# DeltaNet projections all kept in two parts, and one direction's triangular inverses moved to GpSimd

## The chip, the cores and the metric

The kernel runs on one core of a Trainium2 chip. The metric is the device time of one execution in microseconds (us). Below, PE is TensorE, PEld its weight loads, DVE is VectorE, ACT is ScalarE, POOL is GpSimd and SP is SyncE; SP computes nothing here and only issues DMA. TensorE's clock is granted by the chip and has two levels, 1.2 and 2.4 GHz; the profile gives the mean granted clock of a stretch as a share of the full one.

## What is computed

The reference is a trunk of two layers over 256 context tokens and 256 latent tokens of width 1024. Each layer is a half-step SwiGLU feed-forward block (FFN, inner width 2816), a token mixer and a second FFN; the mixer of layer 0 is a gated linear recurrence (LRU), that of layer 1 a bidirectional gated DeltaNet with 8 heads. What matters here is the DeltaNet:

```python
proj = h @ w_in                                   # q, k, v: silu(conv4(.)), z, and a/b for decay and beta
q = l2norm(q) * DN_DK ** -0.5;  k = l2norm(k)
g = -exp(a_log) * softplus(a + dt_bias);  beta = sigmoid(b)
# per direction, chunk of 64 tokens and head:
g_cum = cumsum(g);  decay = exp(g_cum_i - g_cum_j)  for i >= j
a_mat = strictly_lower((k * beta) @ k.T * decay) + I
u, w = solve(a_mat, [v * beta, k * beta * exp(g_cum)])
# then a scan over the chunks with the state s:
v_new = u - w @ s;  o = q_dec @ s + (q @ k.T * decay) @ v_new;  s = s * g_tot + k_dec.T @ v_new
```

There are 64 unit lower triangular matrices a_mat of 64x64 (2 directions, 4 chunks, 8 heads). The output is the latent stream after the last RMSNorm.

## The kernel before

**Weights.** All large products take three matmuls (`mm3`, lines 300 to 303): weight and activation are each the sum of a high part (float32r) and the rest, and hi·hi, hi·lo and lo·hi are added up. A weight tile is 128x1024 floats (512 KB). `Weights` brings it in: SP loads it raw (tile `wr`), ACT makes the high part of each half of 512 columns (`split`, line 165, the trace's CAST), and DVE the low part (line 166). So a tile costs two ACT and two DVE instructions of 128x512. Some later tiles are instead split ahead of time: an entry `keep` in the plan has a tile split during an FFN, SP writes the four pieces to DRAM (tile `kp`), and when its turn comes it is loaded in two parts of 512 KB straight into the pair buffers `wp` (`load`, lines 200 to 212). Before, these loads are issued by POOL (line 209). `PACE["keep"]` says after which inner tiles j of the FFNs 0,1 and 1,0 an entry stands: "1j10 2j10" means after every second one, 22 places in all; `kept_from` and `kept_out` say which tiles use them: the last 16 of the 28 later projections and 4 output tiles.

**The DeltaNet** (`deltanet`). The first four projections (k heads 0 to 3) are made while the normed input arrives. The other 28 are a loop over a list (`SEQ`): k4 to k7, the 8 q heads, then v and z heads mixed in the order of `PACE["seq"]`. A k or v head projects all 512 tokens (two halves of 24 matmuls of 128x256), a q or z head the latent half only. After every six matmuls `tick` runs a few steps of generators that write the remaining work into the program: convolutions, `decays` (from projection number `decay_from`, counted from 0, drained at `decay_to`), and from `keys_from` one step of `keys`. `keys` runs, in this order: per head the key products and decay matrices (`k_rest`), the norms (`norms`), the inverses (`solve`) and the products that put the inverse together (`merge`). `PACE["solve"]` is the number of ticks per step of `solve`.

**The inverses.** `solve` inverts the two 32x32 diagonal blocks of every a_mat. 128 partitions hold 128 blocks of each direction. `N` gets the transposed blocks, `Bc` (its halves are `XI`) starts as the identity, and 31 steps j follow, each of two instructions: tm = column j of N times row j of Bc, and Bc -= tm below row j. Before, both directions are one instruction of 2·m·n elements a partition (n = j+1, m = 31-j), all on DVE (lines 1225 and 1228). Then DVE makes four transposes (lines 1231 and 1232: `A`, `N`, `Bc`), and `merge` starts: 256 matmuls of 32x32 (`pp`, line 1247), ACT copies them out, and for a = 0 and 1 another 128 each (`qq`, line 1266), from which `Yp[a]` is filled. `Yp[0]` takes the memory of the context half of the normed input, which is free after the last v projection (state "contexts"), `Yp[1]` that of the latent half, free after the last projection (state "latents"). Then come the transposes of the keys (`tk`, lines 1131 and 1136), and the scan.

**What sets the order.** In the DeltaNet a scheduler places the instructions of each engine; each engine then runs its own list strictly in order, and an instruction that waits holds up all that stand behind it on its engine. In the FFNs and the LRU the order of PE and SP at least is that of the code.

Of the kernel before, what the change touches and what calls it, by code (L numbers as in the profile page):

```python
# [10 lines left out]
F32 = mybir.dt.float32  # L11
# [4 lines left out]
OP = mybir.AluOpType  # L16
# [11 lines left out]

    "lru": "u0 u1 u2 u3 u4 u5 g0 u6 u7 g1 y0 y1 y2 g2 y3 y4 y5 g3 y6 y7",

    "seq": "qqqqqqqqvvvvzzvzzvvzzvzz",

    "decay_from": 6, "decay_to": 8, "keys_from": 9,

    "steps": 4, "decay_steps": 1, "key_every": 4, "key_steps": 3, "solve": 4, "q_lag": 2, "v_lag": 6, "k_lag": 4,

    "block_split": 1, "mo": 2,

# [2 lines left out]
    "ahead": 1,  # L41


    "kept_from": 12, "kept_out": 4, "keep": "1j10 2j10",
}


# [47 lines left out]
def trunk(ctx, tc, io):  # L95
    nc = tc.nc
# [84 lines left out]
    class Weights:  # L181
# [15 lines left out]
        def load(self, n, half=False):  # L197
            new = []
            while self.plan and len(self.raw) + len(self.ready) < n:
                src, m, *r = self.plan[0]  # L200
                if r == ["p"]:
                    if len(self.raw) + len(self.ready) >= self.limit:
                        break
                    self.plan.popleft()
                    d = self.kept[src]
                    parts = []
                    for a in range(2):
                        w = self.rings["g"].pair()
                        POOL.dma_start(w.both, d[:, a])
                        parts.append(w)  # L210
                    self.raw.append((parts, m, None, None))
                    continue
                if "l" not in self.rings and r == ["l"]:
                    break
                ring = self.rings["g" if r == ["g"] else self.raws[self.nr % len(self.raws)]]
                if ring.used == ring.nraw:
                    break
                if r == ["keep"]:
                    self.kept[src] = self.pool.tile([128, 2, 2, 512], F32R, name=nm("kp"), tag=nm("kp"))
                    r = ["keep", self.kept[src]]  # L220
                    src = io[src[0]][src[1:]]
                self.plan.popleft()
                self.nr += r != ["g"]
                raw = ring.raw()
                ring.used += 1
                nc.sync.dma_start(raw[:, :512 if half else m], src[:, :512] if half else src)
                self.raw.append((raw, m, ring, r))
                if half:
                    new.append((raw[:, 512:m], src[:, 512:]))
            return new  # L230
# [722 lines left out]
    def deltanet(norm, next_norm, sp, hp, pools, done):  # L953
# [258 lines left out]
        def solve():  # L1212
            Nb = pools[1].tile([128, 2, 32, 32], F32, name="N")
            N, XI = ([t[:, dr] for dr in range(2)] for t in (Nb, Bc))
            for dr in range(2):
                DVE.transpose(out=N[dr] if dr == 0 else N[dr].rearrange("p i e -> p e i"), in_=Bc[:, dr])
                x = XI[dr]
                POOL.memset(x, 0.0)
                POOL.memset(x.rearrange("p i c -> p (i c)")[:, ::33], 1.0)
                yield  # L1220
            for j in range(31):
                n, m = j + 1, 31 - j
                tm = pools[1].tile([128, 512], F32, name=nm("tm"), tag="tm", bufs=1)[:, :2 * m * n]
                tm = tm.rearrange("p (d i c) -> p d i c", d=2, c=n)
                DVE.tensor_tensor(tm, Nb[:, :, j + 1:, j:j + 1].to_broadcast([128, 2, m, n]),
                                  Bc[:, :, j:j + 1, :n].to_broadcast([128, 2, m, n]), OP.mult)
                x = Bc[:, :, j + 1:, :n]
                DVE.tensor_tensor(x, x, tm, OP.subtract)
                yield
            for dr, (A, B) in enumerate(((sv("A"), N[0]), (N[1], XI[0]))):  # L1230
                DVE.transpose(out=A.rearrange("p k c -> p c k"), in_=XI[dr].rearrange("p i c -> p c i"))
                DVE.transpose(out=B.rearrange("p k i -> p i k"), in_=XI[dr])
                T[dr], Yd[dr] = (A, B) if dr == 0 else (B, A)
                yield
# [4 lines left out]
        def merge():  # L1239
# [3 lines left out]
            for i0 in (0, 16):  # L1243
# [6 lines left out]
                ACT.copy(pt, pp)  # L1250
                PT.append(pt.rearrange("p (i x) -> p i x", i=16))
                yield
            for a in range(2):
                while a and "latents" not in state:
                    yield
                at = [(dr, c) for dr in range(2) for c in range(2) if a == (c if dr == 0 else 1 - c)]

                Yp.append(hp.tile([128, 32, 128], F32, name=nm("Yp"), tag=f"H{a}", bufs=1))
                (DVE if a else POOL).memset(Yp[a][:, 0:16], 0.0)
                POOL.memset(Yp[a][:, 16:32], 0.0)  # L1260
                for i0 in (0, 16):
                    ii = slice(i0, i0 + 16)
                    qq = bank("qq")
                    for i in range(16):
                        for dr, c in at:
                            PE.matmul(qq[ER[dr, c], i * 32:i * 32 + 32], PT[i0 // 16][IR[dr, c], i, :],
                                      Yd[dr][IR[dr, c], i0 + i, :], start=True, stop=True)
                    for dr, c in at:
                        for k in range(2):
                            dst, src = Yp[a][sub(c, k), ii, sub(c, k)], Yd[dr][sub(c, k), ii]  # L1270
                            if k == 0:
                                ACT.copy(dst, src)
                            else:
                                POOL.tensor_scalar(dst, src, 1.0, 0.0, OP.mult, OP.add)
                    yield
                    for dr, c in at:
                        r = ER[dr, c]
                        dst, src = Yp[a][r, ii, IR[dr, c]], qq[r, :].rearrange("p (i x) -> p i x", i=16)
                        if c:
                            ACT.activation(dst, src, AF.Identity, scale=-1.0)  # L1280
                        else:
                            DVE.tensor_scalar(dst, src, -1.0, None, OP.mult)
                    yield
# [16 lines left out]
        def keys():  # L1300
            live = Pipe()
            for n in range(8):
                while ("k", n) not in state:
                    yield
                live.live.append(k_rest(n))
                for _ in range(PACE["key_every"]):
                    live.tick(PACE["key_steps"])
                    yield
            while live.live:
                live.tick(3)  # L1310
                yield
            yield from norms()
            for _ in solve():
                yield from pause(PACE["solve"])
            while "contexts" not in state:
                yield
            yield from merge()

        later = keys()
# [440 lines left out]
```

## Time and profile before

| | |
|---|---|
| median of 3 runs | 1844.87 us (1843.44 to 1848.66) |
| profiled execution, its own time | 1852.49 us |
| its span, first to last instruction | 1850.7 us |
| mean granted TensorE clock | 0.984 |
| busy: PE, DVE, ACT, POOL | 1782.6, 1314.8, 809.1, 105.7 us |

Places in the trace are us from the span's start. By the rows of PE the FFN 0,1 runs from 594 to 953, the FFN 1,0 from 959 to 1317, the first four DeltaNet projections from 1322, the other 28 from 1349.4 to 1497.0, the pp and qq products to 1514, the scan from 1522, the last FFN from about 1642. A busy PE is no proof of a PE at its peak, because the ends of matmuls are modelled; the distance between starts says more. Durations of DVE instructions that follow each other overlap by some hundredths of a us where the second does not need the first.

### The profile page before, as it was taken

To read this page: it belongs to the slowest core of one execution; us is meant where nothing else is said; L and a number is where in the kernel's file an instruction comes from. 1 tells how busy PE (TensorE), PEld (TensorE's weight loads), DVE (VectorE), ACT (ScalarE), POOL (GpSimd) and SP (SyncE) were. 2 spreads that over 40 slices of the span, in tenths; PEclk is the share of its full clock that TensorE was granted. 3 is DMA by queue.
4 is the path that set the end of the run, shared out by engine and by line. 5 is a ranking of instruction groups with operands and counts; after the bars stand their busy time and mean duration, and the time that the engine had idled before them with its cause. 6 is when DMAs were issued, how large, how long until landed. Compare 5 with 4: busy or idle time off the path is not lost.

```text
span 1850.7 us, 28613 instructions
## 1 busy us (share of the span) xinstructions
PE 1782.6 (96%) x10806; PEld 1544.5 (83%) x10806; DVE 1314.8 (71%) x2694; ACT 809.1 (44%) x1661; POOL 105.7 (6%) x146
## 2 busy tenths in 40 slices
PE   5999999999899999999999999999998989889997
PEld 3788888888778888888898888888997986789997
DVE  7877866797878767667656755545789966976555
ACT  5532222346884433233334322323578333855453
POOL 3100000000000000000000000000017230100000
PEclk9999999999999999999999999999999989989999
DMA  9354645452133666576524765663235540035553
GB/s 346 113 183 158 218 160 172 166 197 80 57 103 127 236 203 219 194 235 213 193 88 151 231 227 199 216 201 127 87 119 167 184 137 1 1 128 178 194 182 106
DMA packets 98058, 300.59 MB, mean 162 GB/s; under 512 B 10880, under 2 KB 20352, under 8 KB 97792
## 3 DMA queue, kind: packets, MB, share of 16 engines
q1 hardware_dynamic: 92160, 277.79, 44.5%
q0 software_dynamic: 5760, 20.97, 3.6%
q8 instruction: 85, 1.39, 0.3%
q14 instruction: 53, 0.43, 0.1%
HBM read 276.70 MB, written 22.02 MB: 161 GB/s over the span
## 4 chain that ended last, share of the span: by engine, by line
PE 80%; DVE 10%; issue 4%; ACT 4%; DMA 2%; POOL 0%; SPq 0%; POOLq 0%; ACTq 0%; DVEq 0%
PE gu L302 14%; PE gu L303 14%; PE gu L301 14%; PE fo L303 4%; PE fo L301 4%; PE fo L302 4%; PE tl L301 4%; PE tl L302 4%; PE tl L303 4%; PE p L1417 1%; DVE u L791 1%; PE p L1406 1%; PE gu L546 1%; PE gu L542 1%; PE p L1386 1%
## 5 line engine op out<-in xcount | busy, mean ns | idle before, releaser
L165 ACT CAST wp<-wr 128x512 fp32r<-128x512 f32 (+1 forms) x689 | 382.4, 607 | 281.9 <-DMA wr<-in_ffn_out_dram 66.1
L166 DVE TENSOR_TENSOR wp<-wr,wp 128x512 fp32r<-128x512 f32 (+1 forms) x689 | 433.4, 675 | 99.7 <-ACT wp L165 95.8
L302 PE MATMUL gu<-hl,wp 128*128 128x512 f32 (+1 forms) x1312 | 479.3, 365 | 8.0 <-DVE hl L505 8.0
L301 PE MATMUL gu<-hh,wp 128*128 128x512 f32 (+1 forms) x1312 | 478.9, 365 | 0.5 <-ACT hh L503 0.5
L303 PE MATMUL gu<-hh,wp 128*128 128x512 f32 (+1 forms) x1312 | 478.4, 365 | 0.0
L407 DVE SCALAR_TENSOR_TENSOR junk<-ar,cb 128x1024 bf16<-128x1024 f32 x224 | 273.7, 1222 | 23.3 <-DMA ar<-in_w_adaT_dram 19.3
L302 PEld LDWEIGHTS gu<-hl,wp 128*128 128x128 f32 x1312 | 247.7, 189 | 48.9 <-DVE hl L505 10.1
L301 PEld LDWEIGHTS gu<-hh,wp 128*128 128x128 f32 x1312 | 247.7, 189 | 41.0 <-ACT hh L503 1.2
L303 PEld LDWEIGHTS gu<-hh,wp 128*128 128x128 f32 x1312 | 249.2, 190 | 38.9
L657 ACT ACTIVATE sg<-gu 128x512 f32<-128x512 f32 (+1 forms) x88 | 47.9, 544 | 366.8 <-PE gu L303 356.8
L659 DVE TENSOR_TENSOR hf<-sg,gu 128x512 f32<-128x512 f32 (+1 forms) x88 | 54.5, 619 | 181.8 <-PE gu L303 130.3
L301 PE MATMUL tl<-hidh,wp 128*128 128x256 f32 (+1 forms) x418 | 139.6, 334 | 0.0
L302 PE MATMUL tl<-hidl,wp 128*128 128x256 f32 (+1 forms) x418 | 139.1, 333 | 0.0
L303 PE MATMUL tl<-hidh,wp 128*128 128x256 f32 (+1 forms) x418 | 139.1, 333 | 0.0
L301 PE MATMUL fo<-hidh,wp 128*128 128x512 f32 (+1 forms) x352 | 127.4, 362 | 0.0
L302 PE MATMUL fo<-hidl,wp 128*128 128x512 f32 (+1 forms) x352 | 127.4, 362 | 0.0
L303 PE MATMUL fo<-hidh,wp 128*128 128x512 f32 (+1 forms) x352 | 127.4, 362 | 0.0
L301 PE MATMUL f<-H,wp 128*128 128x256 f32 x320 | 92.8, 290 | 0.2 <-issue 0.2
L303 PE MATMUL f<-H,wp 128*128 128x256 f32 x320 | 90.9, 284 | 1.0 <-DVE wp L166 1.0
L302 PE MATMUL f<-H,wp 128*128 128x256 f32 x320 | 90.8, 284 | 0.0
L303 PEld LDWEIGHTS tl<-hidh,wp 128*128 128x128 f32 x418 | 79.3, 190 | 7.7
L301 PEld LDWEIGHTS tl<-hidh,wp 128*128 128x128 f32 x418 | 79.0, 189 | 7.9
(322 smaller groups left out, 2827.3 us busy)
## 6 DMA issues: line engine op xcount, KB each, us to landing
wr<-in_ffn_in_dram SPq DMA_DIRECT2D x172, 512.0 KB, 4.7
ar<-in_w_adaT_dram SPq DMA_DIRECT2D x128, 512.0 KB, 3.6
wr<-in_ffn_out_dram SPq DMA_DIRECT2D x64, 512.0 KB, 4.8
kp<-wp SPq DMA_DIRECT2D x80, 256.0 KB, 7.2
wp<-kp POOLq DMA_DIRECT2D x40, 512.0 KB, 4.9
wr<-in_dn_in_dram SPq DMA_DIRECT2D x32, 512.0 KB, 3.9
wr<-in_ffn_out_dram SPq DMA_DIRECT2D x64, 192.0 KB, 3.6
wr<-in_lru_in_dram SPq DMA_DIRECT2D x16, 512.0 KB, 3.9
```

Of the source, the lines that this page charges most:

```text
L165: ACT.copy(dst.hi, src)
L166: DVE.tensor_tensor(dst.lo, src, dst.hi.bitcast(F32), OP.subtract)
L301: PE.matmul(out, w.hi, x.hi, start=start, stop=False)
L302: PE.matmul(out, w.hi, x.lo, start=False, stop=False)
L303: PE.matmul(out, w.lo, x.hi, start=False, stop=stop)
L407: DVE.scalar_tensor_tensor(junk, raw, 1.0, cb[:, v], OP.mult, OP.mult, accum_out=m[:, t % 8, v:v + 1])
L542: PE.matmul(p[:, cols], w.hi, x.hi, start=(k == 0), stop=False)
L546: PE.matmul(p[:, cols], w(k * 128).hi, x.lo, start=False, stop=(k == KD - 1))
L657: ACT.activation(sg[:, cols], P[0][:, cols], AF.Silu)
L659: DVE.tensor_tensor(hf[:, cols], sg[:, cols], P[1][:, cols], OP.mult)
L791: DVE.scalar_tensor_tensor(uv[:, :, a:b], pv[:, :, a + sh:b + sh], cw(j), uv[:, :, a:b], OP.mult, OP.add)
L1386: PE.matmul(p1[:, dr * 128:dr * 128 + 128], KQ[hd][:, 256 + 128 * (ci[dr] - 4):384 + 128 * (ci[dr] - 4)], S[hd][:, dr], start=True, stop=True)
```

## The change

All 28 later projections and 4 output tiles are kept in two parts ("1j110 2j1110" makes 15 + 17 = 32 places), and their loads are issued by SP and not by POOL. The decays start two projections earlier (4, drained at 6) and the keys too (7). `solve` takes one tick a step and not four, and each of its 31 steps is now two instructions on DVE for one direction and the same two on POOL for the other, of m·n elements each. The last v head comes earlier, as projection 27, and "contexts" is set with four z heads still to come. `merge` no longer waits for "contexts" as a whole: only its part a = 0 does. The arithmetic is the same.

```diff
-    "seq": "qqqqqqqqvvvvzzvzzvvzzvzz",
-    "decay_from": 6, "decay_to": 8, "keys_from": 9,
-    "steps": 4, ..., "solve": 4, ...
+    "seq": "qqqqqqqqvvvvzzvvzzvvzzzz",
+    "decay_from": 4, "decay_to": 6, "keys_from": 7,
+    "steps": 4, ..., "solve": 1, ...
-    "kept_from": 12, "kept_out": 4, "keep": "1j10 2j10",
+    "kept_from": 0, "kept_out": 4, "keep": "1j110 2j1110",
...
-                        POOL.dma_start(w.both, d[:, a])
+                        nc.sync.dma_start(w.both.bitcast(F32), d[:, a].bitcast(F32))
...
             for j in range(31):
                 n, m = j + 1, 31 - j
-                tm = pools[1].tile([128, 512], F32, name=nm("tm"), tag="tm", bufs=1)[:, :2 * m * n]
-                tm = tm.rearrange("p (d i c) -> p d i c", d=2, c=n)
-                DVE.tensor_tensor(tm, Nb[:, :, j + 1:, j:j + 1].to_broadcast([128, 2, m, n]),
-                                  Bc[:, :, j:j + 1, :n].to_broadcast([128, 2, m, n]), OP.mult)
-                x = Bc[:, :, j + 1:, :n]
-                DVE.tensor_tensor(x, x, tm, OP.subtract)
+                for dr, E in enumerate((DVE, POOL)):
+                    tm = pools[1].tile([128, 256], F32, name=nm("tm"), tag=f"tm{dr}", bufs=1)[:, :m * n]
+                    tm = tm.rearrange("p (i c) -> p i c", c=n)
+                    E.tensor_tensor(tm, N[dr][:, j + 1:, j:j + 1].to_broadcast([128, m, n]),
+                                    XI[dr][:, j:j + 1, :n].to_broadcast([128, m, n]), OP.mult)
+                    x = XI[dr][:, j + 1:, :n]
+                    E.tensor_tensor(x, x, tm, OP.subtract)
                 yield
...
-            for a in range(2):
-                while a and "latents" not in state:
+            for a, over in enumerate(("contexts", "latents")):
+                while over not in state:
                     yield
...
-            while "contexts" not in state:
-                yield
             yield from merge()
```

Line numbers after line 1220 move by one. On DVE, the end of the inverses before (tm and Bc of the last step, then the four transposes):

```order
L1225 TENSOR_TENSOR tm_13834<-N,Bc 128x62 [waits DVE_49]
L1228 TENSOR_TENSOR Bc<-Bc,tm_13834 128x2x31 [waits DVE_49]
L1231 STREAM_TRANSPOSE A_13837<-Bc 128x32x32 [waits DVE_49]
L1232 STREAM_TRANSPOSE N<-Bc 128x32x32
L1231 STREAM_TRANSPOSE N<-Bc 128x32x32
L1232 STREAM_TRANSPOSE Bc<-Bc 128x32x32 [waits DVE_49]
```

All four stand behind the last step. After the change the same engine has, in its own step j = 11 (n = 12, 240 elements):

```order
L1226 TENSOR_TENSOR tm_13207<-N,Bc 128x231 [waits DVE_49]
L1229 TENSOR_TENSOR Bc<-Bc,tm_13207 128x21x11 [waits DVE_49]
L1226 TENSOR_TENSOR tm_13219<-N,Bc 128x240 [waits DVE_49]
L1232 STREAM_TRANSPOSE N<-Bc 128x32x32 [waits Pool_49]
L1229 TENSOR_TENSOR Bc<-Bc,tm_13219 128x20x12 [waits DVE_49]
L791 SCALAR_TENSOR_TENSOR u_13373<-f_13237,cst,u_13373 128x2x255 [waits Activation_49]
L1226 TENSOR_TENSOR tm_13231<-N,Bc 128x247 [waits DVE_49]
```

One transpose of the other direction (N from its half of Bc) has moved in between: it waits for POOL's last inverse instruction, and behind it stand the rest of step 11, steps 12 to 30, the convolutions of the v heads 2 and 3 and the other three transposes.

On PE, the place of pp before, behind the last matmuls of the last projection (f is a projection's sum, H the normed input, wp a weight pair):

```order
L301 MATMUL f_13767<-H_11449,wp_13625 128x256
L302 MATMUL f_13767<-H_11449,wp_13625 128x256
L303 MATMUL f_13767<-H_11449,wp_13625 128x256
L1247 MATMUL pp_13842<-A_13837,MO_11787 32x32 [waits DVE_49,PE_49]
L1247 MATMUL pp_13842<-A_13837,MO_11787 32x32
L1247 MATMUL pp_13842<-Bc,MO_11788 32x32 [waits DVE_49,Pool_49]
```

And after the change, between the projections 21 (z1) and 22 (v4):

```order
L303 MATMUL f_13541<-H_11603,wp_13240 128x256
L1248 MATMUL pp_13552<-A_13528,MO_11941 32x32 [waits DVE_49]
L1248 MATMUL pp_13552<-A_13528,MO_11941 32x32
L1248 MATMUL pp_13625<-A_13528,MO_11941 32x32 [waits PE_49]
L1248 MATMUL pp_13625<-A_13528,MO_11941 32x32
L301 MATMUL f_13706<-H_11602,wp_13357 128x256 [waits DMAHW7_49,Activation_49]
```

Six matmuls of projection 22 and four transposes of a v head follow, then the other 248 pp matmuls, which wait for the transposed Bc. Behind them stand 330 projection matmuls: the rest of projection 22 and all of 23 to 31. The a = 0 half of qq stands in projection 28, the a = 1 half behind the last projection.

## Rows read from the trace of the kernel before

**Rows 1.** The page: busy time by engine, and the chain that ended last.
```profile
PE 1782.6 (96%) x10806; PEld 1544.5 (83%) x10806; DVE 1314.8 (71%) x2694; ACT 809.1 (44%) x1661; POOL 105.7 (6%) x146
PE 80%; DVE 10%; issue 4%; ACT 4%; DMA 2%; POOL 0%; SPq 0%; POOLq 0%; ACTq 0%; DVEq 0%
```
**Rows 2.** Busy us by stretch: PE, PEld, DVE, ACT, POOL; then clock, DMA, GB/s.
```profile
640.00:970.00 330.00, 329.74 (x1563) 277.52 (x1562) 220.72 (x411) 109.38 (x200) 0.00 (x0) 1.00 0.59 196
970.00:1300.00 330.00, 330.00 (x1508) 275.45 (x1507) 190.10 (x335) 106.23 (x201) 1.52 (x3) 1.00 0.58 191
1377.00:1435.00 58.00, 52.53 (x471) 45.34 (x470) 54.83 (x133) 50.37 (x107) 39.17 (x52) 0.94 0.51 157
1435.00:1498.00 63.00, 62.01 (x589) 59.98 (x587) 61.07 (x109) 22.93 (x69) 20.40 (x34) 1.00 0.67 206
```
**Rows 3.** Chain that ended last, from 1450 to 1500, by line.
```profile
by line: DVE Bc L1228 28.4%; DVE tm L1225 28.1%; DVE u L791 20.0%; DVE A L1231 4.5%; DVE N L1231 4.1%; DVE N L1232 3.9%; DVE Bc L1232 3.6%; PE pp L1247 3.1%; issue 2.3%; ACT u L787 1.2%; ACT vs L1177 0.8%; ACT vs L1178 0.6%; ACTq L1177 0.0%
```
**Rows 4.** DVE in order of time: start, us, line, operation.
```profile
1436.20 2.00 DVE L1216 STREAM_TRANSPOSE N<-Bc 128x1024 f32<-128x1024 f32 x1
...
1490.24 2.25 DVE L1231 STREAM_TRANSPOSE A<-Bc 128x1024 f32<-128x1024 f32 x1
...
1496.38 1.92 DVE L1232 STREAM_TRANSPOSE Bc<-Bc 128x1024 f32<-128x1024 f32 x1
```
**Rows 5.** PE in order of time, around the end of the projections.
```profile
1496.88 0.28 PE L303 MATMUL f<-H,wp 128*128 128x256 f32 x1
1498.44 0.22 PE L1247 MATMUL pp<-Bc,MO 32*32 32x32 f32 x2 [1.11 <-DVE Bc L1232]
...
1514.82 0.63 PE L1131 MATMUL tk<-ident,kq 128*128 128x128 f32 x2
```
**Rows 6.** DVE groups, 1349.3 to 1434.9: count | busy us, mean ns | idle before.
```profile
L166 DVE TENSOR_TENSOR wp<-wr,wp 128x512 fp32r<-128x512 f32 x17 | 12.2, 731 | 0.0
```
**Rows 7.** DVE groups by shape, 1435 to 1498.2.
```profile
L791 DVE SCALAR_TENSOR_TENSOR u<-f,cst,u 128x510 f32<-128x510 f32 x13 | 9.6, 739 | 0.1
L1168 DVE TENSOR_TENSOR qk<-qk,tq 64x256 f32<-64x256 f32 x16 | 6.7, 418 | 0.4
L1225 DVE TENSOR_TENSOR tm<-N,Bc 128x510 f32<-128x510 f32 x2 | 1.4, 691 | 0.1
L1225 DVE TENSOR_TENSOR tm<-N,Bc 128x62 f32<-128x62 f32 x2 | 0.5, 240 | 0.0
```
**Rows 8.** POOL groups of the whole span.
```profile
L209 POOL DMA_DIRECT2D wp<-kp x40 | 22.0, 550 | 46.1 <-PE f L303 40.8 <-DMA wr<-in_dn_out_dram 2.8 <-ACT e L1088 2.1
L1401 POOL TENSOR_TENSOR vn<-oq,vn 128x128 f32<-128x128 f32 x16 | 7.5, 466 | 100.2 <-DVE vn L1429 84.4 <-ACT oq L1399 15.8
L1670 POOL TENSOR_TENSOR o<-o,rs 128x256 f32<-128x256 f32 x3 | 2.1, 728 | 230.3 <-ACT o L1669 230.3
```
**Rows 9.** POOL in order of time, then L1105 of DVE (ns least/median/most; in order).
```profile
1414.75 1.06 POOL L1125 TENSOR_TENSOR gd<-msk,gc 128x512 f32<-128x512 f32 x1
1438.25 0.96 POOL L1218 MEMSET Bc<- 128x1024 f32 x1 [0.82 <-DVE rst L320]
...
L1105 DVE TENSOR_TENSOR qk<-e,msk x16: 404/422/1324, 1390.9 to 1429.1; 64x256 f32<-64x256 f32 x16
```
**Rows 10.** PE in order of time: two starts, 96 projection matmuls apart.
```profile
1350.02 0.28 PE L303 MATMUL f<-H,wp 128*128 128x256 f32 x1
...
1360.90 0.28 PE L303 MATMUL f<-H,wp 128*128 128x256 f32 x1
```
**Rows 11.** PE groups, 1349.3 to 1514.
```profile
L1266 PE MATMUL qq<-N,pt 32*32 32x32 f32 x256 | 7.4, 236 | 3.3 <-issue 3.3
L1184 PE MATMUL tv<-ident,vs 128*128 128x128 f32 x29 | 4.9, 286 | 0.1
```
**Rows 12.** Busy us by stretch, columns as in rows 2, at two places of lower clock.
```profile
1375.00:1385.00 10.00, 9.33 (x71) 8.33 (x71) 9.09 (x19) 6.92 (x20) 3.88 (x3) 0.83 0.54 159
1500.00:1515.00 15.00, 9.45 (x353) 9.07 (x340) 4.91 (x8) 7.99 (x15) 5.31 (x7) 0.57 0.26 81
```

More of the change, by code (lines that the diff above doesn't have):

```diff
@@ L29 @@
     "lru": "u0 u1 u2 u3 u4 u5 g0 u6 u7 g1 y0 y1 y2 g2 y3 y4 y5 g3 y6 y7",
-    "seq": "qqqqqqqqvvvvzzvzzvvzzvzz",
-    "decay_from": 6, "decay_to": 8, "keys_from": 9,
-    "steps": 4, "decay_steps": 1, "key_every": 4, "key_steps": 3, "solve": 4, "q_lag": 2, "v_lag": 6, "k_lag": 4,
+    "seq": "qqqqqqqqvvvvzzvvzzvvzzzz",
+    "decay_from": 4, "decay_to": 6, "keys_from": 7,
+    "steps": 4, "decay_steps": 1, "key_every": 4, "key_steps": 3, "solve": 1, "q_lag": 2, "v_lag": 6, "k_lag": 4,
     "block_split": 1, "mo": 2,
```

## Prediction

> **What bounds the kernel now.** I read the page first: PE is busy 96% of the span and carries 80% of the chain that ended last, DVE 10% [rows 1]. Such shares mix stages, so I then took windows by stage. In both FFNs in which tiles are split ahead PE is busy 329.7 and 330.0 of 330 us, DVE 220.7 and 190.1 us, DMA 0.59 and 0.58 [rows 2]: there PE alone sets the time. In the DeltaNet loop PE is full again up to 1498 (62.0 of 63), but DVE is as full (61.1 of 63) [rows 2], and in that stretch the chain runs on DVE's inverses, not on PE [rows 3]. Yet the wait behind them is small: DVE's last transpose ends at 1498.3 [rows 4], and PE, whose last projection matmul starts at 1496.88, waits 1.11 us for it before pp [rows 5]. So projections and inverses run side by side and end together; a change gains only if it shortens both, and loses if it puts one behind the other. Both orders below matter for that: each engine runs its list strictly in order.
>
> **What the new order does.** On DVE one transpose of POOL's half stands in DVE's own step 11 and waits for POOL's last inverse instruction. Behind it are 39 of DVE's 62 half-size operations, six convolutions and three transposes. On PE the products pp stand after projection 21 and wait for the last of these transposes; 330 projection matmuls stand behind them. What ran side by side becomes a line: POOL's inverses, then the rest of DVE's, then the rest of PE's projections. I time this line link by link, in places of the trace of before.
>
> **Link 1, when N is ready.** The second N is done at 1436.20 + 2.00 = 1438.2 [rows 4]. Ahead of it DVE loses 17 splits, 12.2 us [rows 6], and three convolutions of 0.74 [rows 7] that now stand behind, 2.2. Starting the decays earlier makes them wait about 2 us more for a/b and for the cumulated decays, an estimate. 1438.2 − 12.2 − 2.2 + 2 = **1426**. DVE was nearly full there (54.8 of 58 [rows 2]), so its lost work does bring it forward; if half of the idle 3 us stays I get 1422, if the new waits are double and part of the splits' time is not recovered, 1430.
>
> **Link 2, POOL's inverses.** POOL fills its identity first, about 1.3 us (0.96 for the large fill [rows 9], 0.3 for the small one and the handoff). Then come 62 operations, each needing the one before. Step n has n(32 − n) elements, summed over 31 steps 5,456, twice that for two operations: 10,912 elements a partition. POOL took 0.466 us for 128 elements and 0.728 for 256 [rows 8]: 2.05 ns an element and 0.204 fixed. That gives 62 × 0.204 + 10,912 × 0.00205 = 12.6 + 22.4 = 35.0. For the handoff between dependent operations I add 62 × 0.06 = 3.7. An operation of 512 elements took 1.06 us [rows 9], 0.2 less than this line, perhaps as its input is repeated, as in tm here; for 31 such operations, most of them shorter, I take off 2.5. So 36. While DVE works beside it, both slow down: a DVE operation of 0.42 us took up to 1.32 beside POOL's [rows 9]. DVE has 23 half-size operations before it comes to the waiting transpose; at 0.2 us each they hold POOL 5 us. Taken: **41 us**, bounds 33 (no slowing, repeated inputs cheap) and 46 (each of the 23 costs POOL its full 0.35, two more us of handoff). POOL ends at 1426 + 1.3 + 41 = **1468.3**. DVE is at the waiting transpose long before: 16 operations of 0.42 [rows 7], 23 half-size ones of together 8 us, seven convolutions of 0.74 make some 20 us, 1446. It then stands about 20 us.
>
> The Trainium skill, page "SBUF — State Buffer", section "Who interferes with whom", has a stricter rule that speaks against this change: a DVE instruction with both inputs in SBUF and a GpSimd instruction hold an exclusive lock on a shared port pair, and whichever is second waits until the other is done. The 1.32 beside 0.42 us agrees with it, the median of 0.42 shows only that most had no neighbour. By the rule in full the 23 operations would cost POOL 8 us and not 5, and the sum below would be 3 us more; without any lock it would be 5 less.
>
> **Link 3, the rest of DVE.** The waiting transpose is 2.2 [rows 4]. Half-size operations by the rows of before: 240 ns for 62 elements, 691 for 510 [rows 7], so 1.0 ns an element and 0.18 fixed. The 39 left hold 7,460 elements: 39 × 0.19 + 7,460 × 0.00104 = 15.2. Six convolutions of 0.66 from start to start, 4.0. Three transposes from 1.92 to 2.25 [rows 4], 6.2, less 0.2 overlap. Together **27.4**; Bc is ready at **1495.7** (before: 1498.3).
>
> **Link 4, PE behind it.** pp 3 us. Projection matmuls follow at (1360.90 − 1350.02) / 96 = 0.1133 us [rows 10]: 330 × 0.1133 = 37.4. The v heads in them bring five more groups of transposes (29 took 4.9 us [rows 11]; some 15 here) 2.5. The first half of qq about 2 (all 256 hold PE 7.4 us busy, overlapping [rows 11]). PE has stood some 45 us, and after a pause the clock is low: it was 0.57 where pp and qq ran thinly, and 0.83 in a stretch beside waits, 3.4 us of ten at half clock, which lose half of that [rows 12]. I take 2, bounds 0 and 4. Together **46.9**, to 1542.6; the second half of qq, 2, and tk can start at **1544.8**. Before it started at 1514.82 [rows 5]. So **+30 us**. Scan and last FFN are not touched.
>
> **Edits costed at nothing.** Twelve more tiles are split ahead, four in FFN 0,1 and eight in FFN 1,0: 24 more DVE splits of 0.72 [rows 6], as many on ACT, 12 loads of 0.5 MB and stores of 1 MB. A PE at 330 of 330 with DVE at 67% and 58% hides them [rows 2]; without that cover they cost 24 × 0.68 = 16 us. Loads on SP: 28 MB in some 150 us is under 200 GB/s, and 206 was moved at a share of 0.67 [rows 2]. The first one, for k4, may come up to 1 us late; range only. POOL loses 40 issues, 22.0 us [rows 8], that would otherwise stand in its list.
>
> **The sum.** The profiled execution took 1852.49 us, 7.6 above the median shown; its own 1852.49 + 30 is 1882.5. The stage shift does not depend on which execution it is, so from the median: 1844.87 + 30 = **1875 us**.
>
> **Rivals.**
> *Faster: the inverses hidden.* If pp's inputs are ready when PE comes to them (about 1443, after 26 halves of 24 matmuls and some 23 us of other work from 1349.4), tk comes when PE's own work is done and DVE's tail no longer counts: at about 1493, −22 us, **1823**. The point that decides: Bc ready by 1495.7 − 30 = 1465.7 would be no change. DVE's own work after N is 20 + 27.4 us, 1426 + 47.4 = 1473, with no wait for POOL at all; so it would need N eight us earlier too. For it: the rates of POOL stand on few rows. 3%.
> *POOL as quick as the order supposes.* If POOL is done when DVE reaches the transpose, it takes 20 us, 0.3 an operation. Bc is ready at 1473, 22 us earlier: +8, **1853**. Against it: 0.466 for 128 elements [rows 8], and the mean here is 176. 7%.
> *The splits come on PE's path.* +16 on top, **1891**. Against it: the windows of 330 us. 5%.
> *The change doesn't do what it says.* The 32 places are just what 28 projections and 4 output tiles need, so no tile falls back to raw loading; the remaining chance, 2%, is for no change by causes that cancel.
>
> **How the numbers follow.** The forecast has 83%. Its bounds: N −4 and +4, POOL −8 and +5, DVE ±1, PE −3 and +5, FFN up to 3, the first load 1. Not all fall together, so I take the root of the squares, about −10 and +9, and widen each side to 15 and 14 for what the rows don't price: **1860 to 1889**, which leaves the first rival, POOL as quick and the splits outside. A measurement of this kernel can tell about 0.3%, 5.5 us, from no change. Slower by more: forecast, POOL as quick and splits, 95%. Within it 2%, faster 3%.
>
> **What would show it right or wrong.** Right: PE idle over 40 us in one piece before pp, ended by DVE's transposes; DVE idle near 20 us, ended by a POOL inverse operation; POOL's inverses 36 to 46 us long; pp's main part at 1492 to 1500; tk at 1540 to 1550; the FFN windows still 330 of 330. Wrong: pp with no wait, or POOL ready before DVE comes to the transpose; or tk within 10 us of 1515 (all places shift alike if earlier stages do).

## The result, and the profile after

The changed kernel takes **1901.37 us** (median of 4 runs, 1894.6 to 1908.48) against 1844.36 before (now 4 runs as well): 1.0299 times as long, 95% interval 1.0272 to 1.0326, or 57 us slower. The direction and the main mechanism were forecast; the size, 30 us with a range up to 1889, was not. Its profiled execution took 1898.01 us, 45.5 more than the one of before, which was 8 us above its own median. One execution of the run e9 below, of 4079.62 us, is a slow one and left out of its median.

The page of the changed kernel, busy time and the shares of the chain that ended last, against [rows 1]:

```profile
PE 1789.6 (94%) x10806; PEld 1545.2 (81%) x10806; DVE 1307.2 (69%) x2694; ACT 813.7 (43%) x1664; POOL 114.6 (6%) x168
PE 67%; DVE 12%; DMA 7%; issue 6%; ACT 4%; POOL 2%; SPq 1%; POOLq 0%; ACTq 0%; DVEq 0%
```

The instructions are nearly the same in number; what grew is waiting. DMA went from 2% to 7% of the chain, a first sign that something happens outside the DeltaNet, where the weights are written ahead. I cut the span at four places of PE that both traces have: the first DeltaNet projection, the first tk, the first matmul of the last FFN, the last matmul.

| stage, us | before | after | difference |
|---|---|---|---|
| start to the DeltaNet's first projection | 1322.3 | 1335.0 | +12.7 |
| from there to tk (loop, pp, qq) | 192.5 | 225.3 | +32.8 |
| tk to the last FFN (scan, output) | 136.0 | 143.0 | +7.0 |
| last FFN | 192.6 | 185.5 | −7.1 |

**The loop** is the predicted line. DVE of the changed kernel in order of time (start, us, line, operation); the last row is the end of DVE's part:

```profile
1465.65 0.83 DVE L1226 TENSOR_TENSOR tm<-N,Bc 128x240 f32<-128x240 f32 x1
1483.92 2.00 DVE L1232 STREAM_TRANSPOSE N<-Bc 128x1024 f32<-128x1024 f32 x1 [17.44 <-POOL Bc L1229]
1485.74 0.45 DVE L1229 TENSOR_TENSOR Bc<-Bc,tm 128x240 f32<-128x240 f32 x1
...
1508.14 1.92 DVE L1233 STREAM_TRANSPOSE Bc<-Bc 128x1024 f32<-128x1024 f32 x1
```

In step 11 DVE stops for 17.44 us until POOL's last inverse operation is done:

```profile
1483.64 0.25 POOL L1229 TENSOR_TENSOR Bc<-Bc,tm 128x31 f32<-128x31 f32 x1
```

It then works through the rest until 1510.06; before, the last transpose ended at 1498.3 [rows 4]. What that does to PE, from its waits between 1340 and 1575 (us in total, times, longest):

```profile
PE tv L1184 <- ACT vs L1178: 18.6, 1, 18.6
PE pp L1248 <- DVE A L1232: 9.7, 1, 9.7
PE tq L1159 <- DVE qk L1168: 5.4, 2, 5.2
```

The first wait I had not named: PE does not reach pp. It stops before, at the transposes of a v head whose convolution stands behind DVE's waiting transpose. So PE stands 28.3 us in two pieces, where the prediction had over 40 in one piece before pp: PE was behind already, and came to the v head at 1471 only. From 1435 to 1450 it was busy 7.45 of 15 us at a granted clock of 0.61:

```profile
1435.00:1450.00 15.00, 7.45 (x115) 6.70 (x113) 13.31 (x33) 8.97 (x28) 8.45 (x19) 0.61 0.20 70
```

By the line that loss costs nothing here, since PE would have waited for Bc all the same; e15 below, where PE comes sooner and waits longer, bears it out. Between 1465 and 1510 PE is busy 15.9 us of 45, at a mean granted clock of 0.70 (columns as in [rows 2], where PE was busy 62 of the last 63 us of the loop):

```profile
1465.00:1510.00 45.00, 15.89 (x118) 15.04 (x116) 26.36 (x51) 5.93 (x19) 16.45 (x32) 0.70 0.26 88
```

**FFN 0,1**, which I had costed at nothing, lost 12.7 us. PE's waits from 594 to 1340 show two of a kind that the kernel before had none of; below them the longest wait that PE had before in the same stages:

```profile
PE tl L301 <- ACT hidh L165: 4.7, 1, 4.7
PE fo L301 <- ACT hidh L165: 2.2, 1, 2.2
```
```profile
PE gu L546 <- DVE hl L505: 0.7, 1, 0.7
```

The first two are at the last inner tile of a half, whose hidden activation comes late. Why shows DVE's list ahead of the second one:

```profile
906.99 1.22 DVE L407 SCALAR_TENSOR_TENSOR junk<-ar,cb 128x1024 bf16<-128x1024 f32 x1
...
909.30 1.22 DVE L407 SCALAR_TENSOR_TENSOR junk<-ar,cb 128x1024 bf16<-128x1024 f32 x1 [1.08 <-DMA ar<-in_w_adaT_dram]
...
910.57 1.22 DVE L407 SCALAR_TENSOR_TENSOR junk<-ar,cb 128x1024 bf16<-128x1024 f32 x1
...
911.72 0.68 DVE L659 TENSOR_TENSOR hf<-sg,gu 128x512 f32<-128x512 f32 x1
```

DVE's list is strictly in order. The hidden activation (hf) stands behind products on the modulation weights (junk), these wait for loads (ar) that SP issues in order behind loads of raw weights and stores of kept tiles, and DVE's splits wait in turn for ACT (84.4 us in this FFN, 76.0 before). SP itself waited mostly at the raw loads, for DVE's splits (215.6 us, 205.6 before), and 6.7 us at the stores. Which member of this ring starts the delay is not shown; that the four extra tiles do is shown by e1. PE waits 6.9 us in all; after each wait twelve matmuls stand 0.43 us apart in place of 0.23, about half the rate (the granted clock from 913.0 to 919.4 is 0.50, the lower of the two levels), and lose some 3 us more.

### The profile page after: what moved, and what is told of

It reads as the page before. It is cut to its first block, busy times and chain, and to the rows that moved or that the text cites. A ratio compares the mean times of both kernels' runs of the same rounds, so it can differ in the third digit from the quotient of the medians.

```text
span 1896.0 us, 28820 instructions
## 1 busy us (share of the span) xinstructions
PE 1789.6 (94%) x10806; PEld 1545.2 (81%) x10806; DVE 1307.2 (69%) x2694; ACT 813.7 (43%) x1664; POOL 114.6 (6%) x168
## 4 chain that ended last, share of the span: by engine, by line
PE 67%; DVE 12%; DMA 7%; issue 6%; ACT 4%; POOL 2%; SPq 1%; POOLq 0%; ACTq 0%; DVEq 0%
PE gu L302 10%; PE gu L301 10%; PE gu L303 10%; DMA kp<-wp 4%; PE fo L302 4%; PE fo L303 4%; PE fo L301 4%; PE tl L302 3%; PE tl L301 3%; PE tl L303 3%; DVE wp L166 2%; DMA ar<-in_w_adaT_dram 2%; PE p L1416 2%; DVE junk L407 1%; DVE hl L505 1%
## 5 line engine op out<-in xcount | busy, mean ns | idle before, releaser
L407 DVE SCALAR_TENSOR_TENSOR junk<-ar,cb 128x1024 bf16<-128x1024 f32 x224 | 273.9, 1223 | 21.0 <-DMA ar<-in_w_adaT_dram 17.1
L301 PEld LDWEIGHTS tl<-hidh,wp 128*128 128x128 f32 x418 | 79.7, 191 | 13.1 <-ACT hidh L165 5.2
L165 ACT CAST hidh<-hf 128x512 fp32r<-128x512 f32 (+1 forms) x88 | 49.9, 567 | 94.3 <-DVE hf L659 94.3
```

The source lines that it names most:

```text
L165: ACT.copy(dst.hi, src)
L301: PE.matmul(out, w.hi, x.hi, start=start, stop=False)
L407: DVE.scalar_tensor_tensor(junk, raw, 1.0, cb[:, v], OP.mult, OP.mult, accum_out=m[:, t % 8, v:v + 1])
```

## The experiments

Times are medians; the ratio is to the kernel before, with its 95% interval. The last table gives all stages.

**e1: the four extra places moved out of FFN 0,1.**
```diff
-    "keep": "1j110 2j1110",
+    "keep": "1j10 2j1",
```


> The changed kernel with one edit: FFN 0,1 splits ahead after every second inner tile (11 places, as in the kernel before) and FFN 1,0 after each (21 used). Theory 'queue': in the changed kernel the four extra kept tiles of FFN 0,1 push the adaptive-weight loads back on SP and the products on them back on DVE, so that the hidden activations come late twice (PE waited 2.2 and 4.7 us and then ran at a lower clock, 13.6 us in all); with 11 places there and all others in FFN 1,0, PE waits for no hidden activation, the DeltaNet starts 13 us earlier, and the time is 1888 us. Rival 'work': each extra split tile costs its time wherever it is done, about 1 us; then the loss moves to FFN 1,0 and the time stays at 1901 us.


1889.93 us, 1.0252 (1.0218 to 1.0287). The DeltaNet starts at 1323.3, the two waits are gone, and FFN 1,0 hides 21 tiles without a wait. "Queue" holds, at 11.4 us.

**e2: no transpose can stand ahead of DVE's last step.**
```diff
-            for dr, (A, B) in enumerate(((sv("A"), N[0]), (N[1], XI[0]))):
+            for dr, (A, B) in enumerate(((sv("A"), N[1]), (N[0], XI[0]))):
```


> The changed kernel with the two N buffers of the last transposes swapped, so that none of them can stand ahead of DVE's last inverse step. Theory 'line': DVE's 17.4 us wait in step 11 goes; DVE ends its own steps while POOL still works, both end at 1485 to 1489, four transposes of 2 us follow, Bc is ready near 1497 in place of 1510, and the time falls by 13 us to 1888 us. Rival 'ports': DVE and POOL slow each other so much when both work all the time that Bc is not ready before 1506; then the time falls by less than 5 us. Second rival 'PE behind': PE's other waits hold tk back anyway; the time stays at 1901 us though Bc comes early.


1888.39 us, 1.024 (1.0218 to 1.0263): 13.0 less, as "line" says. Bc is ready 161.8 us after the DeltaNet's start, in the changed kernel 175.1. Behind the q heads PE now has one long wait, at pp:

```profile
PE pp L1248 <- DVE A L1232: 16.7, 1, 16.7
```

**e3: pp behind the last projection.**
```diff
+            while "latents" not in state:
+                yield
             yield from merge()
```


> The changed kernel with the products pp put behind the last projection, as in the kernel before; DVE's order keeps the transpose that waits for POOL. Theory 'line': PE then works through the 330 projection matmuls while DVE waits, so its 28 us of idle time before pp and most of the low clock behind it go; the projections end near 1517, after Bc at 1510, tk starts near 1531 in place of 1560, and the time falls by about 29 us to 1872 us. Rival 'contention': PE's projections are slow because POOL and DVE hold what PE needs (sums not read, pairs not free); then PE still stands for DVE, in the convolutions behind the waiting transpose, and the time falls by less than 12 us.


1886.61 us, 1.0229 (1.0205 to 1.0252): half of what "line" expected, and won in another place. The loop got only 2.8 us shorter than its 225.3; PE's waits there:

```profile
PE tv L1184 <- ACT vs L1178: 22.4, 2, 18.7
```

The v head holds PE as long as DVE waits for POOL, whether pp stands there or not. That is what the rival "contention" described, though the time fell by more than its 12 us. The gain is in the scan, 134.5 us in place of 143.0 (below).

**e4: the inverses back on DVE, all else as changed** (lines 1223 to 1229 as in the kernel before).


> The changed kernel with the inverses as before, both directions in one DVE instruction; pp still stands in projection 22. Theory 'line': what counts is only when Bc is ready, because pp stands early on PE. After N at 1444 DVE needs 6.7 us of key products, 32.5 us of inverses, about nine convolutions and small work of 8 us and 8.4 us of transposes, so Bc is ready near 1500 in place of 1510, and the time falls by about 10 us to 1891 us; PE still stands 20 us before pp. Rival 'GpSimd is the loss': inverses on GpSimd are the whole cause of the loss in the DeltaNet; then the 33 us go and the time is 1868 us.


1890.89 us, 1.0256 (1.0226 to 1.0286): 10.5 less, as "line" says; Bc is ready 166.4 us after the DeltaNet's start, and PE waits 20.3 us before pp. In the profiled executions both the loop and the time to Bc are 8.7 us shorter. GpSimd is not the whole loss: with pp in projection 22 any late Bc costs PE: in the changed kernel, e1, e2 and e4 tk comes 50.2 to 51.7 us after Bc.

**e5 and e6: the weights' part alone on the kernel before**, with the change's 15 + 17 places (e5) and with 11 + 21 (e6).
```diff
-    "kept_from": 12, "kept_out": 4, "keep": "1j10 2j10",
+    "kept_from": 0, "kept_out": 4, "keep": "1j110 2j1110",     e5
+    "kept_from": 0, "kept_out": 4, "keep": "1j10 2j1",         e6
-                        POOL.dma_start(w.both, d[:, a])
+                        nc.sync.dma_start(w.both.bitcast(F32), d[:, a].bitcast(F32))
```


> The kernel before with only the weights' part of the change: all 28 later projections kept, 15 + 17 places, loads by SP. Theory 'queue': the same two late hidden activations in FFN 0,1 as in the changed kernel, 12 to 14 us; in the DeltaNet DVE is free of 17 splits, PE's small waits fall by 1 to 4 us; 1855 us. Rival 'harmless alone': the FFN loss needs something else of the change; then 1841 to 1844 us.

> The kernel before with all 28 later projections kept, but 11 places in FFN 0,1 as before and 21 in FFN 1,0, loads by SP. Theory 'queue': no late hidden activation in either FFN, so 11 to 14 us less than with 15 + 17 places; 1842 us, within 0.3% of the kernel before, since the DeltaNet is bound by PE once DVE has the room. Rival 'DVE was the bound': with DVE free of the splits Bc comes 12 us earlier and PE's waits of 7 us in the loop go; 1836 us.


e5: 1850.36 us, 1.0031 (1.0013 to 1.0049). e6: **1839.62 us, 0.9979 (0.9967 to 0.999)**, the fastest of this study and a little faster than the kernel before. The 10.7 us between them are FFN 0,1 (PE waits 3.4 and 3.2 us for hidh in e5). In both the loop to tk gains: 187.2 and 186.3 us against 192.5. So the kept weights are worth some 6 us in the DeltaNet, and the change's 15 + 17 places lose twice that in FFN 0,1.

**e7 and e8: all holds of the line undone, e7 with pp behind the projections, e8 with pp in projection 28** (e1 and e2 with e3; e1 and e2 with merge waiting for "contexts").


> The changed kernel with three edits together: 11 + 21 places, the buffers of the last transposes swapped (no DVE wait in step 11), pp behind the last projection. Theory 'two holds': in the changed kernel PE is held twice, by pp and by the v transposes behind DVE's wait, so that each edit alone leaves the other hold (with late pp alone PE still waited 18.7 us for a v head); with both gone the projections end near 1504 and tk starts near 1519, the scan takes 135 us to the last FFN as with late pp alone, and the time is 1847 us, some 54 us below the changed kernel. Rival 'early decays cost': PE waits for DVE near 1437 to 1450 (5.4 us for the q products and more) stay and the POOL inverses slow DVE; then 1855 to 1862 us.

> The changed kernel with 11 + 21 places, the swapped buffers, and pp waiting for the context half as in the kernel before, so that with the new order of heads it stands in projection 28, three and a half projections before the end. Theory 'two holds': Bc is ready near 1485, about when PE gets there, so PE waits under 4 us, pp and half of qq run inside the projections at the full clock, tk starts near 1512. If the scan then takes 142 us as in all kernels with early pp, the time is 1848 us; if it takes 135 us as with late pp, 1841 us. Rival: Bc comes later than PE by 10 us or more; 1855 us.


e7: 1865.55 us, 1.0106 (1.0084 to 1.0128). e8: 1867.3 us, 1.0126 (1.0106 to 1.0146). 36 us of 57 are back in e7, not 54: the rival "early decays cost" was nearer. e8 lies above all that was expected, and not by its rival either: Bc was in time (PE waits for no transpose at pp), but PE itself came to projection 28 some 20 us late. So costs are left that have nothing to do with the wait in step 11. e9 to e11 look for them.

**e9: e7 with "solve": 4; e10: e7 with the decays at 6, 8, 9.**


> Run e7 (the changed kernel with 11 + 21 places, swapped buffers, late pp) with the inverses paced as before, one step per four ticks in place of one. Theory 'DVE's order': with one step per tick the inverses stand ahead of the convolutions of the v heads on DVE, and PE waited 7.9 and 2.9 us at v transposes near 1465 and 1480, then ran at a lower clock; spread out again, these waits go and the time falls from 1866 to about 1856 us; the wait of 5.8 us near 1427 stays. Rival 'GpSimd': POOL's use of the shared memory port delays DVE whatever the pace; the waits stay and so does the time, within 3 us.

> Run e7 with decays and keys starting where they did before (6, 8, 9 in place of 4, 6, 7), inverses still one step a tick. Theory 'DVE's order': begun earlier, the key work takes DVE in front of the q heads' convolutions and ends in POOL's writes of Bc and the N transposes, on which PE stood 5.8 us near 1427 and ran at 0.62 of the clock; from 1400 to 1440 it was busy 28 of 40 us, in run e6 36 of 40. Started as before, these 8 us and some clock come back: 1856 us. Rival 'no room': the same work collides with the inverses later; 1866 us as in e7.


e9: 1865.33 us, 1.0112 (1.0083 to 1.0142), no gain: the pace is not it. e10: 1849.24 us, 1.0021 (1.0005 to 1.0037): the earlier decays cost 16 us in e7.

**e11: e6 with one direction on POOL and e2's buffers; e13: the same, POOL's 62 operations left out; e14: e6 with the early decays.**


> Run e6 (the kernel before with all weights kept, 11 + 21 places, loads by SP) with one direction's inverses on POOL, swapped buffers, all paces and the order of heads as before. Theory 'order, not GpSimd': moving the inverses in itself costs nothing; DVE loses some 16 us of work, PE's small waits at the end of the loop (3 us) may go; 1836 to 1840 us, against 1839.6. Rival 'GpSimd': POOL at 0.54 us an operation against DVE's 0.26, and the port they share, make Bc late; 1848 us or more.

> Run e11 with GpSimd's 62 inverse operations left out (that direction's blocks stay the identity, so part of the computation is missing); DVE's list and PE's list stay as in e11. Theory 'port': DVE's 62 half-size operations take 21 to 23 us in place of 31.5, the convolutions behind them come up to 9 us earlier, PE's waits of 9.1 us for v heads go, and the time falls from 1857.7 to 1838 to 1843 us. Rival 'order': DVE's operations are as long as before or the waits stay for the place of the convolutions in the list; 1852 us or more.

> Run e6 (all weights kept, 11 + 21 places, inverses on DVE as before) with the decays and keys started at 4, 6, 7 in place of 6, 8, 9. Theory 'early decays cost by themselves': DVE takes the key work ahead of the q heads' convolutions, PE waits near 1427 as in e7; the time rises from 1839.6 by 10 to 16 us to 1850 to 1856 us. Rival 'only with GpSimd': without POOL beside it DVE has the room; 1838 to 1842 us.


e11: 1857.73 us, 1.0076 (1.0048 to 1.0104), 18 more than e6: I was wrong, the move itself costs. e13: 1845.54 us, 1.0002 (0.9989 to 1.0015): 12 of the 18 come back when POOL's operations are gone, between "port" and "order". PE's waits for v heads go from 9.1 to 4.5 us (e11, then e13); that the order of the list has the rest is likely, but was not tried:

```profile
PE tv L1184 <- ACT vs L1178: 9.1, 3, 5.2
```
```profile
PE tv L1184 <- ACT vs L1178: 4.5, 2, 4.3
```

The two inverse lines on DVE between 1436 and 1495 (count | busy us, mean ns | idle before), in e6 (whole operations), e11 (half-size, POOL beside) and e13 (half-size, alone):

```profile
L1228 DVE TENSOR_TENSOR Bc<-Bc,tm 128x62 f32<-128x62 f32 (+15 forms) x31 | 16.3, 526 | 0.8
L1225 DVE TENSOR_TENSOR tm<-N,Bc 128x62 f32<-128x62 f32 (+15 forms) x31 | 16.2, 524 | 0.7
```
```profile
L1229 DVE TENSOR_TENSOR Bc<-Bc,tm 128x31 f32<-128x31 f32 (+15 forms) x31 | 16.1, 521 | 0.9
L1226 DVE TENSOR_TENSOR tm<-N,Bc 128x31 f32<-128x31 f32 (+15 forms) x31 | 15.4, 496 | 0.9
```
```profile
L1229 DVE TENSOR_TENSOR Bc<-Bc,tm 128x31 f32<-128x31 f32 (+15 forms) x31 | 10.6, 342 | 0.9
L1226 DVE TENSOR_TENSOR tm<-N,Bc 128x31 f32<-128x31 f32 (+15 forms) x31 | 10.6, 341 | 0.9
```

Alone, half the elements take 21.2 us in place of 32.5. Beside POOL the halves take 31.5: what POOL takes over DVE loses again, 10.3 us of the 11.3. POOL loses less. In the changed kernel its last 31 operations, with DVE standing still, took 16.1 us, the 31 of the same sizes before them, beside DVE, 17.5; all 62 took 33.6 there and 35.0 in e11, some 3 more than twice 16.1. This is the rule that the prediction cited (the Trainium skill, page "SBUF — State Buffer", section "Who interferes with whom"): the trace agrees that two such streams hinder each other, and the 31 DVE operations of e11 that took over 0.5 us each end 0.10 to 0.29 us behind one of POOL's. It does not agree with a lock for the whole of each operation: by themselves the two streams take 21.2 and about 32 us, 53 in all, and in e11 both ran within 44. Which of them pays is what I had the wrong way round.

e14: 1854.62 us, 1.0054 (1.0038 to 1.0071), 15.0 more than e6. The early decays cost without GpSimd too. The stretch from 1400 to 1440 in e6, then in e14 (busy us of PE, PEld, DVE, ACT, POOL; clock):

```profile
1400.00:1425.00 25.00, 24.28 (x241) 20.82 (x239) 24.72 (x67) 22.04 (x48) 15.64 (x23) 1.00 0.54 184
1425.00:1440.00 15.00, 12.16 (x156) 10.39 (x156) 14.34 (x36) 7.54 (x24) 6.24 (x11) 1.00 0.25 87
```
```profile
1400.00:1425.00 25.00, 20.47 (x202) 17.53 (x202) 23.12 (x66) 24.55 (x50) 11.59 (x17) 1.00 0.50 174
1425.00:1440.00 15.00, 9.61 (x121) 8.92 (x120) 13.37 (x32) 6.98 (x22) 4.74 (x8) 0.56 0.13 43
```

Begun two projections earlier, the key work fills ACT (24.55 of 25 us), PE loses 6 us of busy time and then runs at a granted clock of 0.56; and N is hardly earlier for it (ready at 1436.2 in e14, 1438.3 in e6, where the DeltaNet began 1.4 us later).

**e12: e6 with "solve": 2, by which pp moves into projection 30.**


> Run e6 with the inverses paced at two ticks a step, all on DVE; pp then stands in projection 30, ahead of the end, and the scan's order on PE changes as in all kernels with early pp: 237 changes between kinds of matmul in the scan in place of 221 for the same 640 matmuls. Theory 'changes of kind set the scan': each costs about 0.46 us, so the scan's matmuls take 100.3 us in place of 92.8, while pp and qq, 17.5 us after the projections in e6, mostly at a low clock, take some 8 us less; the sum is 1839 to 1841 us, no gain. Rival 'early pp is a gain if Bc is in time': the scan stays at 93 us; 1832 us. Second rival: Bc is not in time in projection 30; over 1845 us.


1847.42 us, 1.0016 (0.9998 to 1.0034). The second rival: Bc came 4.4 us late for PE. The scan took 143.1 us to the last FFN, as "changes of kind" says. PE in order of time in the scan, e6 and then e8:

```profile
1536.40 0.43 PE L1389 MATMUL p<-S,kq 128*64 128x128 f32 x2
1536.76 0.49 PE L1406 MATMUL p<-r,Yp 128*128 128x128 f32 x2
1537.18 0.43 PE L1389 MATMUL p<-S,kq 128*64 128x128 f32 x2
1537.54 0.49 PE L1417 MATMUL p<-vs,kt 64*128 64x128 f32 x4
1537.96 0.43 PE L1389 MATMUL p<-S,kq 128*64 128x128 f32 x2
```
```profile
1556.04 0.43 PE L1390 MATMUL p<-S,kq 128*64 128x128 f32 x2
1556.41 0.48 PE L1418 MATMUL p<-vs,kt 64*128 64x128 f32 x2
1556.82 0.43 PE L1390 MATMUL p<-S,kq 128*64 128x128 f32 x2
1557.18 0.49 PE L1407 MATMUL p<-r,Yp 128*128 128x128 f32 x2
1557.60 0.49 PE L1418 MATMUL p<-vs,kt 64*128 64x128 f32 x2
1558.02 0.43 PE L1390 MATMUL p<-S,kq 128*64 128x128 f32 x2
```

A group of one kind takes about 0.4 us from start to start, with two matmuls or with four. Ten matmuls are four groups in e6 (1.56 us) and five in e8 (1.98). Over the 640 matmuls of the scan I count 221 changes of kind in the kernels with late pp and 237 in those with early pp, and 92.3 to 92.8 us against 100.0 to 100.6. The scheduler orders the scan in the light of what it has placed ahead, so moving pp reorders a stage that the change does not touch. The Trainium skill, page "TensorEngine Tiling (Array Packing)", section "Key Properties", says that a change of tiling mode drains the engine; the rows, in which the array shapes 128*64, 128*128 and 64*128 alternate, agree so far that each group costs about 0.42 us in both orders (92.3 us for 222 groups, 100.2 for 238); the drain itself they do not show. With what else differs it is some 0.48 us for each of the 16 changes.

**e15: the changed kernel with only the decays as before.**


> The changed kernel with only the decays and keys started as before (6, 8, 9); its pp then stands in projection 24 in place of 22, with 56 us less work behind it than... that is 52 projection matmuls fewer (6 us). Theory 'line': N was ready at 1432.0 with late and 1432.4 with early decays in otherwise equal kernels, so the line POOL, DVE, PE starts at the same time; only the 6 us of projections that now stand before pp are won; 1895 us. Rival 'additive': the 16 us that the same edit gave in e10 come back here too; 1885 us.


1883.51 us, 1.0205 (1.0184 to 1.0225): 18 less, in size nearer to "additive". Of that the loop gives 10.3 in the profiled execution (225.3 to 215.0), and there the line explains it. Counted from the DeltaNet's start N is ready after 109.8 us and Bc after 174.6, in the changed kernel after 109.2 and 175.1: POOL's and DVE's part of the line is where it was. But in the trace 230 projection matmuls stand behind the main part of pp and not 330; I had counted 52 fewer, and it is 100. So tk comes 40.4 us behind Bc in place of 50.2. PE reaches pp sooner, and waits there:

```profile
PE pp L1248 <- DVE A L1232: 26.6, 1, 26.6
```

The FFN 0,1, where nothing was edited, gives another 6.1 (the DeltaNet starts at 1328.9). In the five other kernels with 15 + 17 places, whose FFN 0,1 is the same, the DeltaNet started between 1331.5 and 1336.3, so this part seems to differ from execution to execution; with one trace of each kernel that is not shown.

All stages in the profiled executions, us: start of the DeltaNet; to tk; to the last FFN; the last FFN.

| kernel | median | start | to tk | scan | last FFN |
|---|---|---|---|---|---|
| before | 1844.4 | 1322.3 | 192.5 | 136.0 | 192.6 |
| after | 1901.4 | 1335.0 | 225.3 | 143.0 | 185.5 |
| e1 places moved | 1889.9 | 1323.3 | 226.0 | 142.8 | 185.4 |
| e2 buffers | 1888.4 | 1334.0 | 213.5 | 141.8 | 192.2 |
| e3 late pp | 1886.6 | 1336.3 | 222.5 | 134.5 | 186.0 |
| e4 DVE inverses | 1890.9 | 1331.5 | 216.6 | 143.3 | 192.6 |
| e5 weights only | 1850.4 | 1334.3 | 187.2 | 134.4 | 185.0 |
| e6 same, moved | 1839.6 | 1324.4 | 186.3 | 134.5 | 185.0 |
| e7 e1+e2+e3 | 1865.6 | 1323.4 | 209.9 | 136.1 | 192.5 |
| e8 pp in 28 | 1867.3 | 1322.7 | 205.8 | 141.8 | 185.5 |
| e9 e7, pace 4 | 1865.3 | 1322.7 | 210.4 | 137.4 | 185.4 |
| e10 e7, decays | 1849.2 | 1322.3 | 195.2 | 135.0 | 192.1 |
| e11 e6, POOL | 1857.7 | 1322.8 | 200.5 | 135.5 | 185.0 |
| e12 e6, pp in 30 | 1847.4 | 1322.9 | 193.0 | 143.1 | 185.2 |
| e13 e11, no work | 1845.5 | 1322.4 | 191.7 | 133.6 | 185.1 |
| e14 e6, decays | 1854.6 | 1323.0 | 203.3 | 135.4 | 185.3 |
| e15 decays back | 1883.5 | 1328.9 | 215.0 | 140.7 | 184.7 |

## Why the prediction was right and wrong

- **The line and its links: right.** From N to tk each link came within 3 us. POOL's inverses, forecast 41: 38.4 (1445.50 to 1483.89). DVE's rest, 27.4: 26.1. PE behind it, 46.9 + 2 (which is 1544.6 and not 1544.8): 50.2. Loop to tk, +30: +32.8. e2, e4 and e15 moved the end by what the line says. The sign for PE, over 40 us idle in one piece, did not come: 28.3 in two.
- **Link 1, "N ready at 1426": missed by 5.5 us.** Counted from the DeltaNet's start N was ready after 109.2 us, before after 115.9: 6.7 earlier and not 12.2. The step that failed is "DVE was nearly full there, so its lost work does bring it forward". Up to the second N transpose DVE's busy time fell from 101.6 to 83.1 us, but its idle time rose from 12.3 to 24.2. In the changed kernel 6.0 of that are a wait for a/b, where I had 2. Later decays would not have helped: in e15 N was ready after 109.8, and DVE waited 9.7 us for ACT's part of the convolutions in place of the 6.0. What DVE no longer did turned largely into waiting.
- **Link 2, who pays for the port: wrong, though the sum held.** I let POOL pay 5 us. It paid 1.4 in the changed kernel and some 3 in e11, and DVE, where it works beside POOL throughout, 10. In the changed kernel DVE's stall hid this.
- **"Edits costed at nothing": the step that failed first, and the largest.** From PE's 330 of 330 us [rows 2] and DVE's 67% I concluded that twelve more tiles are hidden. Shares of busy time say nothing of when in DVE's list the hidden activation comes: 11.4 us by e1, 10.7 by e5 against e6. The rival at 5%, at 1891 us the nearest of all, had nearly the size (16 us) but by DVE's throughput, and it set the loss in both FFNs; FFN 1,0 hid even 21 places.
- **"Scan and last FFN are not touched": wrong for the scan.** It became 7.0 us longer, with 16 more changes of kind of matmul; moving pp back alone (e3) takes 8.5 us off it. The new order could have been read there as well.
- **The sum.** 30 + 11.4 to 12.7 (FFN) + 2.8 (loop) + 7.0 (scan) is 51 to 53 of 57 us; the last 4 lie between the profiled executions and the medians, of which no trace shows the cause.
- **The faster rival** (inverses hidden) is far off, as argued. e7, e8 and e11 show it would not have been reached by order alone: the move to GpSimd and the early decays each cost 15 to 18 us by themselves on e6. These costs need not add up in the changed kernel: there PE waits for Bc, and what delays PE ahead of that wait costs nothing by itself; the early decays cost there through the place of pp (e15).

## What to carry to other kernels

An engine's share of busy time doesn't tell whether more work on it is hidden; look at what stands in its in-order list ahead of the one instruction that the bound engine waits for, and at the queue that feeds those. Moving half of a two-input SBUF loop from DVE to GpSimd gave DVE 1 us of 32.5 here, because its operations took 10.3 us longer beside GpSimd's. And where a scheduler orders the program, read the new order of every later stage, also of those that the diff leaves alone.

## What was not expected of the hardware

The last FFN takes 184.7 to 186.0 us in twelve of these profiled executions and 192.1 to 192.6 in five, and no edit touches that FFN; in the four windows read, two of each kind, the granted clock is 1.00. Its windows of 100 us, before and e6:

```profile
1700.00:1800.00 100.00, 100.00 (x852) 100.00 (x851) 58.42 (x106) 48.43 (x99) 0.00 (x0) 1.00 0.55 184
```
```profile
1695.00:1795.00 100.00, 100.00 (x885) 100.00 (x884) 59.97 (x109) 49.61 (x101) 0.00 (x0) 1.00 0.57 189
```

852 matmuls against 885 in the same time, 3.7% slower, and the granted clock doesn't show it. What sets it is open. Each kernel has one trace, so that it differs between executions of the same kernel is likely but not shown. It could be most of the 8 us by which the profiled execution of before lay above its median, and is a warning against reading a few us out of a single pair of profiles.
